# Modulation products issued a whole piece at a time, the half that lands last in front

## The chip, the cores and the metric

The kernel runs on one core of a Trainium2 chip. The metric is the device time of one execution in microseconds (us); runs of the kernel before and of the changed kernel are compared by it. The profile is one execution, taken by the hardware profiler, with the instructions of each engine: TensorE (PE for its matmuls, PEld for its weight loads), VectorE (DVE), ScalarE (ACT), GpSimd (POOL) and SyncE (SP), whose queue issues nearly all DMAs here.

## The reference

One layer of a hybrid backbone over 256 latent tokens of width 2048, with 256 context tokens beside them. What matters here is the modulation at its start:

```
mod   = silu(c)     @ ada_w + ada_b        # for the latent tokens
mod_c = silu(c_ctx) @ ada_w + ada_b        # for the context tokens
sh1, sc1, g1, sh2, sc2, g2 = split(mod, 6) # each 2048 wide
h  = rmsnorm(x)   * (1 + sc1)  + sh1
hc = rmsnorm(ctx) * (1 + csc1) + csh1
q, k, v, f, hy = split(h @ w_in)
kc, vc         = split(hc @ w_in[k and v columns])
```

After that come attention, a Fourier branch and a long-convolution branch, an output projection, a gated MLP and a final norm. They stand after the part that is changed here.

## The kernel before

The first stage computes `sh1` and `sc1` for both vectors at once and, from them, the projection to keys and values. The 2048 input columns are 16 tiles of 128 (`KT`), cut into five blocks of 2, 2, 4, 4 and 4 tiles (`CFG["blocks"]`). For each block the stage needs the modulation of that block's tiles (A and B, lines 502 and 503), then `hprep` (line 517) makes `h` and `hc` of these tiles as a high and a low part (`hx_hi`, `hx_lo`, `hc_hi`, `hc_lo`), and `group` (line 545) adds the block's share of keys and values. A block has four groups; the pieces of the next block's modulation are traced a quarter ahead of each group (lines 614 to 617).

A *piece* is what `piece(m, q)` returns, with `m` for scale (0) or shift (1). It loads two half-megabyte tiles of `ada_w` (`ada_load`, line 467, through the weight stream `load`, line 266), which are its two halves, and multiplies them with the two vectors `s_t`, which stand as the columns of a 128 x 32 stationary operand. The moving operand is 512 columns wide in blocks of four tiles and 256 in blocks of two. A piece of 512 columns has four products, a half two; a piece of 256 columns has eight, a half four. The product of input tile `kt` writes strip `kt % 4` of a PSUM bank, which is 32 partitions high; the four strips are added at the end, after the last piece of a scale or shift (lines 493 to 497: ScalarE copies the bank to `adasb`, TensorE transposes it, VectorE reduces it). A shift or scale takes four pieces at 512 columns and two at 256.

In all there are 4 pieces for block 0, which are worked in the start-up, 4 for block 1 and 8 each for blocks 2, 3 and 4.

The order on each engine is fixed when the kernel is built. The planner follows the order in which the program traces the instructions, but an instruction whose operands are not there yet by its estimate is passed by later ones that are ready. An edge between two instructions of one engine (`tc.issue_after`) says which is issued first; it adds no semaphore wait. On the chip each engine then runs its queue in that order, and an instruction waits on semaphores for what it reads. A product waits for the load of the half that it reads.

The buffers: eight half-megabyte tiles in `w1.raw`, which the modulation weights share with the projection weights (`w_kv_t`) and with the side products' weights (`ada_col_t`, line 351 on VectorE, which compute four other parts of the modulation and are drawn in by `pump`), and three more in `a_raw`. SP issues the loads in one order, and a load waits until its buffer is free, that is, until what read it is done.

## Time and profile before

| | us |
|---|---|
| median of three runs | 1309.89 |
| the three runs | 1307.58, 1309.89, 1340.22 |
| the profiled execution | 1307.8 |
| its span on the core | 1306.0 |
| TensorE busy (matmuls) | 1282.9 |
| VectorE busy | 887.3 |
| ScalarE busy | 557.7 |

The products of line 489 appear in the profile as `mi_ps<-raw,s_t` or, for block 0, `acc_ps<-raw,s_t`; the shape `128*32` is that of the stationary operand, `128x512` or `128x256` that of the moving one. The projection's matmuls appear on line 162, as `acc_ps<-hx_hi,w_hi` and the like. In a timeline row stand the start, the duration from the first record's start to the last one's end, the engine, the line, the operation, what it writes and reads, its shape and the number of records that were merged into the row, and in brackets the idle time of the engine before it and what ended that. Matmuls overlap in the pipeline, so the distance from one start to the next says more than a duration.

### The profile page before, as it was taken

How to read it: one execution, taken by the hardware profiler on the slowest of the kernel's cores; microseconds unless marked ns; L12 is line 12 of the kernel's file. 1: busy time of each engine (PE TensorE's matmuls, PEld its weight loads, DVE VectorE, ACT ScalarE, POOL GpSimd, SP SyncE). 2: the span in 40 equal slices, each digit the busy share in tenths (PEclk: the TensorE clock that was granted, in tenths of full speed). 3: DMA queues.
4: the chain of work that ended last, by engine and by line, in shares of the span. 5: the costliest groups of instructions: out<-in, count | busy, mean ns of one | idle time of the engine just before them, and what ended most of it. 6: DMA issues, size and time to landing. Idle time of an engine off the chain costs nothing.

```text
span 1306.0 us, 24498 instructions
## 1 busy us (share of the span) xinstructions
PE 1282.9 (98%) x10290; PEld 1195.4 (92%) x10290; DVE 887.3 (68%) x1301; ACT 557.7 (43%) x736; POOL 0.9 (0%) x7
## 2 busy tenths in 40 slices
PE   9899999999998999999999999999999999999997
PEld 5666787999998988999999999999999999999997
DVE  5435577977999897987767776744445555555563
ACT  3531223133443565555544444433334444454453
POOL 0000000000000000000000000000000000000000
PEclk9999999999999999999999999999999999999999
DMA  9976787988686875756777777855556656556541
GB/s 361 361 261 233 268 320 308 350 278 297 225 321 245 336 245 194 240 189 229 246 271 257 260 244 272 290 194 194 194 194 194 194 194 194 194 194 194 194 163 65
DMA packets 94015, 315.28 MB, mean 241 GB/s; under 512 B 16080, under 2 KB 16336, under 8 KB 93264
## 3 DMA queue, kind: packets, MB, share of 16 engines
q1 hardware_dynamic: 93328, 312.65, 68.8%
q8 instruction: 80, 1.31, 0.4%
q10 hardware_dynamic: 576, 1.07, 0.2%
q14 instruction: 31, 0.25, 0.1%
HBM read 311.58 MB, written 2.10 MB: 240 GB/s over the span
## 4 chain that ended last, share of the span: by engine, by line
PE 84%; DVE 9%; DMA 2%; ACT 2%; issue 2%; SPq 1%; DVEq 0%; ACTq 0%
PE acc_ps L162 77%; PE mi_ps L162 3%; PE mi_ps L489 3%; DVE raw L351 3%; DVE w_lo L174 2%; DMA raw<-in_ada_col_t 1%; SPq L636 1%; PE mi_ps L170 1%; DMA pack<-in_pack 0%; SPq L268 0%; DVE kT L570 0%; DVE v_t L570 0%; ACT w_hi L173 0%; ACT kT L461 0%; DVE Y L755 0%
## 5 line engine op out<-in xcount | busy, mean ns | idle before, releaser
L173 ACT CAST w_hi<-raw 128x1024 fp32r<-128x1024 f32 x376 | 380.5, 1050 | 514.1 <-PE acc_ps L162 467.4
L174 DVE TENSOR_TENSOR w_lo<-raw,w_hi 128x1024 fp32r<-128x1024 f32 x376 | 448.0, 1221 | 216.1 <-ACT w_hi L173 215.0
L162 PE MATMUL acc_ps<-h_hi,w_hi 128*128 128x256 f32 x1408 | 388.2, 276 | 0.5 <-ACT h_hi L256 0.5
L162 PE MATMUL acc_ps<-h_lo,w_hi 128*128 128x256 f32 x1408 | 388.6, 276 | 0.0
L162 PE MATMUL acc_ps<-h_hi,w_lo 128*128 128x256 f32 x1408 | 388.5, 276 | 0.0
L162 PEld LDWEIGHTS acc_ps<-h_hi,w_hi 128*128 128x128 f32 x1408 | 264.1, 188 | 0.7 <-ACT h_hi L256 0.7
L162 PEld LDWEIGHTS acc_ps<-h_lo,w_hi 128*128 128x128 f32 x1408 | 264.3, 188 | 0.0
L162 PEld LDWEIGHTS acc_ps<-h_hi,w_lo 128*128 128x128 f32 x1408 | 264.3, 188 | 0.0
L162 PE MATMUL acc_ps<-yh,w_lo 128*128 128x256 f32 x704 | 194.3, 276 | 0.0
L162 PE MATMUL acc_ps<-yh,w_hi 128*128 128x256 f32 x704 | 194.3, 276 | 0.0
L162 PE MATMUL acc_ps<-yl,w_hi 128*128 128x256 f32 x704 | 194.3, 276 | 0.0
L351 DVE SCALAR_TENSOR_TENSOR raw<-raw,s_row 128x1024 f32<-128x1024 f32 x128 | 154.4, 1220 | 35.1 <-DMA raw<-in_ada_col_t 35.0
L162 PE MATMUL acc_ps<-hx_hi,w_hi 128*128 128x256 f32 x512 | 143.6, 284 | 2.0 <-ACT hx_hi L256 2.0
L162 PE MATMUL acc_ps<-hx_hi,w_lo 128*128 128x256 f32 x512 | 142.9, 282 | 2.4 <-DVE w_lo L174 2.4
L162 PE MATMUL acc_ps<-hx_lo,w_hi 128*128 128x256 f32 x512 | 143.6, 282 | 0.0
L162 PEld LDWEIGHTS acc_ps<-yh,w_hi 128*128 128x128 f32 x704 | 132.2, 188 | 0.0
L162 PEld LDWEIGHTS acc_ps<-yl,w_hi 128*128 128x128 f32 x704 | 132.2, 188 | 0.0
L162 PEld LDWEIGHTS acc_ps<-yh,w_lo 128*128 128x128 f32 x704 | 132.2, 188 | 0.0
L162 PEld LDWEIGHTS acc_ps<-hx_hi,w_hi 128*128 128x128 f32 x512 | 96.5, 190 | 8.6 <-ACT hx_hi L256 4.0
L162 PEld LDWEIGHTS acc_ps<-hx_hi,w_lo 128*128 128x128 f32 x512 | 96.6, 190 | 6.7 <-issue 3.6
L162 PEld LDWEIGHTS acc_ps<-hx_lo,w_hi 128*128 128x128 f32 x512 | 97.3, 190 | 3.1 <-issue 2.2
L681 ACT ACTIVATE ga<-acc_ps,pack 128x256 f32<-128x256 f32 x44 | 23.7, 559 | 37.6 <-PE acc_ps L162 31.6
(237 smaller groups left out, 1532.9 us busy)
## 6 DMA issues: line engine op xcount, KB each, us to landing
raw<-in_ffn_t SPq DMA_DIRECT2D x264, 512.0 KB, 4.3
raw<-in_ada_col_t SPq DMA_DIRECT2D x128, 512.0 KB, 5.1
raw<-in_ada_t SPq DMA_DIRECT2D x64, 512.0 KB, 5.3
raw<-in_w_in_t SPq DMA_DIRECT2D x48, 512.0 KB, 5.8
raw<-in_w_kv_t SPq DMA_DIRECT2D x32, 512.0 KB, 5.9
raw<-in_w_out_t SPq DMA_DIRECT2D x32, 512.0 KB, 4.7
x_in<-in_xT SPq DMA_DIRECT2D x8, 256.0 KB, 5.4
kT<-in_c_tok SPq DMA_DIRECT2D x1, 2048.0 KB, 12.1
```

The lines of the kernel that those rows point to most:

```text
L162: return nc.tensor.matmul(ps, lhsT, rhs, start=start, stop=stop, skip_group_check=True)
L170: nc.tensor.transpose(ps, src, ident[:n, :n])
L173: nc.scalar.copy(hi, src)
L174: TT(lo, src, hi.bitcast(F32), op=ALU.subtract)
L351: STT(r, r, 1.0, s_row[:, h * NA : (h + 1) * NA], op0=ALU.mult, op1=ALU.mult, accum_out=sums_[:, f, h : h + 1])
L489: nc.tensor.matmul(ps[32 * j : 32 * j + 32, :w], s_t[:, kt, :], raws[(kt - n2 * q) // (n2 // 2)][:, kt % (n2 // 2), :], start=kt < 4, stop ...
L636: nc.sync.dma_start(half[:, hd], src)
L681: nc.scalar.activation(dst, ps, AF.Identity, bias=b, scale=w1_)
```

## The change

The products of a piece are issued in another order and tied together. The first product of the second half (the one that is loaded later) comes first; it waits for that half's load. All others of the piece, the rest of the second half and then the first half, are put behind it by `issue_after`. As the strips are now begun in another order, the flag that starts a strip's sum goes to the first product that touches the strip (`begun`), and the flag that ends it to the last ones. The loads, the buffers and the number of products stay as they are.

```diff
-                    for kt in range(n2 * q, n2 * q + n2):
+                    nh = n2 // 2
+
+                    def product(i):
+                        kt = n2 * q + i
                         j = kt % 4
-                        nc.tensor.matmul(ps[32 * j : 32 * j + 32, :w], s_t[:, kt, :], raws[(kt - n2 * q) // (n2 // 2)][:, kt % (n2 // 2), :], start=kt < 4, stop=kt >= KT - 4, skip_group_check=True)
+                        begun = st_.setdefault((m, "strips"), set())
+                        fresh = j not in begun
+                        begun.add(j)
+                        return nc.tensor.matmul(ps[32 * j : 32 * j + 32, :w], s_t[:, kt, :], raws[i // nh][:, kt % nh, :], start=fresh, stop=q == last_q and i in ends, skip_group_check=True)
+
+                    ends = range(4) if n2 == 8 else range(n2)
+                    last_raw = product(nh)
+                    with tc.issue_after(last_raw.ins):
+                        for i in [*range(nh + 1, n2), *range(nh)]:
+                            product(i)
                     if q < last_q:
                         return
```

## The prediction

> **What bounds the kernel now.** I read the page first, then the modulation products (line 489) by stretch, then single bursts of them in the timeline, then the loads that feed them.

> ```profile
> span 1306.0 us, 24498 instructions
> ...
> PE 1282.9 (98%) x10290; PEld 1195.4 (92%) x10290; DVE 887.3 (68%) x1301; ACT 557.7 (43%) x736; POOL 0.9 (0%) x7
> ...
> PE   9899999999998999999999999999999999999997
> ...
> DVE  5435577977999897987767776744445555555563
> ```

> TensorE is the bound: from the third slice on (a slice is 32.7 us) it is never below 80%, nearly always at 90% or more. What shortens TensorE's queue there can shorten the kernel, unless another engine steps in. The products stand in the first 215 us; the next view counts their records alone (the columns are the stretch, its length, TensorE's busy time and records, the clock, the DMA share, GB/s).

> ```profile
> 50.00:68.00 18.00, 5.11 (x64) 1.00 0.83 316
> 72.00:114.00 42.00, 16.83 (x64) 1.00 0.75 257
> 114.00:124.00 10.00, 4.21 (x16) 1.00 0.58 182
> 124.00:215.00 91.00, 13.46 (x112) 1.00 0.77 298
> ```

> One product is two records: the code issues 32 products of 256 columns for block 1 and the first row has 64. So 64, 64 + 16 and 112 records are 4, 20 and 7 bursts of 8, 4 and 16, sizes that the timeline shows. The 80 records of 72 to 124 us cost 21.04 us of busy time, the 112 after them 13.46: small bursts are dear. Why, one burst of four shows:

> ```profile
> 94.64 0.39 PE L162 MATMUL acc_ps<-w_lo,hx_hi 128*128 128x512 f32 x1
> 94.87 0.40 PE L162 MATMUL acc_ps<-w_hi,hx_lo 128*128 128x512 f32 x1
> 95.19 1.05 PE L489 MATMUL mi_ps<-raw,s_t 128*32 128x512 f32 x4
> 96.17 0.50 PE L162 MATMUL acc_ps<-w_hi,hx_hi 128*128 128x512 f32 x1
> 96.51 0.39 PE L162 MATMUL acc_ps<-w_lo,hx_hi 128*128 128x512 f32 x1
> ```

> Two projection matmuls follow one another in 0.23 us (94.64 to 94.87). From 94.87 to 96.51 two such steps should take 0.46; they take 1.64. The burst costs **1.18 us**: it enters 0.09 late, leaves 0.11 late, and ends with a tail that nothing fills.

> **The change, part by part.** What each step costs or saves:

> *Half pieces joined, 512 columns.* A whole piece uses all four strips of 32 output rows; a half uses two. What eight records (four products on four strips) take shows where two whole pieces are issued together. The first row below is cut at 131.20, so it holds the first piece only; the others are the whole burst.

> ```profile
> 130.63 1.06 PE L489 MATMUL mi_ps<-raw,s_t 128*32 128x512 f32 x8
> ```

> ```profile
> 130.43 0.28 PE L162 MATMUL acc_ps<-hc_hi,w_lo 128*128 128x256 f32 x1
> 130.63 1.92 PE L489 MATMUL mi_ps<-raw,s_t 128*32 128x512 f32 x16
> 132.49 0.38 PE L162 MATMUL acc_ps<-hx_hi,w_hi 128*128 128x256 f32 x1
> 132.71 0.28 PE L162 MATMUL acc_ps<-hx_lo,w_hi 128*128 128x256 f32 x1
> ```

> Four products on four strips last 1.06 us, two products on two strips 1.05. So the second half of a piece is free if it is issued beside the first: a joined piece costs 1.18 + 0.01 = 1.19 instead of 2 x 1.18 = 2.36, which saves **1.17**. The new order (third, fourth, first, second) still touches four different strips. The 20 bursts of four are 10 pairs: 11.7 us.

> [...]

> *Half pieces joined, 256 columns.*

> ```profile
> 50.63 0.28 PE L162 MATMUL acc_ps<-hx_lo,w_hi 128*128 128x256 f32 x1
> 50.84 0.64 PE L489 MATMUL mi_ps<-raw,s_t 128*32 128x256 f32 x8
> 51.41 0.38 PE L162 MATMUL acc_ps<-hx_hi,w_lo 128*128 128x256 f32 x1
> 51.63 0.29 PE L162 MATMUL acc_ps<-hx_hi,w_hi 128*128 128x256 f32 x1
> ```

> Here a half already uses four strips. From 50.63 to 51.63 two steps of 0.115 would do (256 columns, half of the 0.23 of 512); the burst costs 1.00 - 0.23 = 0.77. A whole piece of this width stands in the start-up:

> ```profile
> 24.69 1.50 PE L489 MATMUL acc_ps<-raw,s_t 128*32 128x256 f32 x22
> ...
> 30.06 1.05 PE L489 MATMUL acc_ps<-raw,s_t 128*32 128x256 f32 x10
> ...
> 34.67 1.07 PE L489 MATMUL acc_ps<-raw,s_t 128*32 128x256 f32 x16
> ```

> Sixteen records last 1.07, eight 0.64: 0.43 more. Joined 0.77 + 0.43 = 1.20 against 1.54 saves 0.34; four pairs, 1.4 us.

> *Start-up (block 0).* The third piece is split: six records ride in the burst of 22, ten come at 30.06. Whole, it would make 16 + 16: 0.43 off the first burst (1.50 to 1.07), 0.02 onto the second. After the first burst TensorE waits for ScalarE's copy of an earlier sum, so I take 0, with 0.4 as the upper bound.

> *The seven bursts of 16.* They are whole pieces already, two at a time; only their inner order changes. 0.

> *Cover that goes.* One removed burst, the one at 114.80, stands where TensorE waits for the next block's input:

> ```profile
> 114.22 0.66 PE L170 MATMUL mi_ps<-pack,adasb 128*128 128x128 f32 x4 [0.32 <-ACT adasb L493]
> 114.80 1.05 PE L489 MATMUL mi_ps<-raw,s_t 128*32 128x512 f32 x4
> ...
> 115.33 0.91 ACT L256 ACTIVATE hx_hi<-ht,B 128x256 fp32r<-128x256 f32 x2 [1.17 <-DVE B L503]
> ...
> 115.89 0.39 PE L162 MATMUL acc_ps<-hx_hi,w_hi 128*128 128x256 f32 x1
> ```

> The matmul at 115.89 waits for the activation of 115.33 whatever the burst does, so its removal uncovers an idle time of the same 1.1 us. That pair saves 0.1: minus 1.1.

> *The added wait.* A piece's first product now waits for the half that lands last, and behind it in TensorE's queue stand the other products and all projection matmuls. What they would wait:

> ```profile
> 56.95 2.31 SPq L268 DMA_DIRECT2D raw<-in_ada_t  x4
> ```

> ```profile
> DMA to landing us min/median/max: 3.4/4.3/8.7
> ```

> ```profile
> 72.34 1.05 PE L489 MATMUL mi_ps<-raw,s_t 128*32 128x512 f32 x4
> ...
> 78.42 1.05 PE L489 MATMUL mi_ps<-raw,s_t 128*32 128x512 f32 x4
> ```

> The four loads issued at 56.95 to 59.3 feed the four bursts from 72.34 to 78.42, so each is used 15 to 19 us after its issue. The second row is for loads of modulation weights issued between 50 and 125 us: they land within 8.7 us at worst. The wait has some 7 us to spare: 0.

> *Buffers held longer.* The first half's buffer is freed with the second half's burst instead of its own, which is 1.9 us later (93.31 against 95.19):

> ```profile
> 93.31 1.05 PE L489 MATMUL mi_ps<-raw,s_t 128*32 128x512 f32 x4
> ```

> ```profile
> SPq L268 <- PE mi_ps L489: 104.3, 29, 10.1
> ```

> SP's queue, in which all weight loads stand in one order, does wait for these releases (104.3 us in 29 waits up to 330 us), so loads will start later by up to 1.9. The 7 us spare covers it; I take 0 and price the opposite as the third rival. No load is moved in the program.

> *After it.* The gain arises before 124 us; does it reach the end?

> ```profile
> 125.00:222.00 97.00, 97.00 (x652) 77.69 (x651) 65.94 (x119) 22.50 (x33) 0.00 (x0) 1.00 0.79 307
> 222.00:285.00 63.00, 63.00 (x452) 58.73 (x452) 59.52 (x92) 16.18 (x18) 0.00 (x0) 1.00 0.90 325
> ```

> TensorE (first count) is full in both stretches, VectorE (third) has 31 us free in the first and only 3.5 in the second, DMA 10%. Both stretches are driven by releases of TensorE and VectorE, so they should shift as a whole.

> Sum: 11.7 + 1.4 + 0 - 1.1 = **12.0 us** less. Upper end: 0.4 in the start-up, and 1.7 if the two pieces of each of the five groups with bursts of four came together as later ones do (two joined pieces at 1.19 are 2.38, a burst of 16 costs 2.28 - 0.23 = 2.05 between 130.43 and 132.71: 0.33 x 5): 14.1. Lower end with one more burst found to be cover: 10.9; adding a pair whose order the planner keeps apart, 9.7. The profiled execution took 1307.8 us (span 1306.0, 1.8 around it), so it would take 1295.8. The median of three before is 1309.9, the lowest 1307.6; an ordinary run lies 0 to 2 above the profiled one, so I say **1297**.

> **The rivals.**

> *Gain given back later.* Between 222 and 285 us VectorE is busy 59.52 of 63 us, in queue order with side products that wait for loads. If it can't start 12 us earlier, up to half of the gain is lost: 1302. Against: its 31 free us in the stretch before. Chance 0.17.

> *The halves don't run beside one another.* Then a joined piece costs 1.18 + 0.87 = 2.05 (0.87 is what the burst of 16 has over the burst of four), a pair saves 0.31, ten 3.1, and with 1.4 and less 1.1 the time is 1304. The x8 row of 1.06 us speaks against it. Chance 0.05.

> *It does not do what it says.* The edges order products, they do not make them neighbours; if the planner still puts projection matmuls between them, the bursts stay as many: 1308 to 1310. Chance 0.06.

> *Slower: TensorE's queue stops at the front product.* The place is lines 489 and 268 between 50 and 215 us. The longer hold delays SP's next loads by 1.9 us for each of the 14 joined pieces; if these add up instead of being caught by the spare time, 26.6 us of TensorE waiting stand against 12 saved: 1322. It decides from the point at which the 7 us spare is used up, that is after four pieces whose delay isn't recovered. For it: SP does wait for line 489, 104.3 us in all. Against: in 50 to 124 us the DMA engines are busy 58 to 83%, so they can catch up. [...] Chance 0.11, of which 0.04 for more than 2% (a delay twice as long).

> *More than forecast*, below 1291, by changes of order that I can't read here: 0.05, of which 0.02 beyond 2%.

> **How the numbers follow.** The forecast, 1291 to 1299 (1307.8 less 14.1 or 9.7, and 1 to 3 us for what differs between runs), has 0.56; the first rival 0.17, the second 0.05, the third 0.06, slower 0.11, more 0.05. The range from 1290 to 1308 holds the forecast, the first two rivals and parts of the third and of the last: 8 in 10. A measurement here tells about 2% from no change (26 us: below 1284 or above 1336). All but 0.02 below and 0.04 above lies within: faster 0.02, same 0.94, slower 0.04.

> **What would show it.** Between 50 and 68 us bursts of 16 records instead of 8, and after that bursts of eight or 16 and none of four; 14 bursts fewer; a joined 512-column burst of about 1.06 us; an idle TensorE of about 1 us ahead of block 2's first projection; the first projection matmul after what is now the burst at 130.63 some 12 us earlier; the stretch now at 222 to 285 as long as before. Wrong would be: TensorE waiting for a load at line 489, bursts of four left, joined bursts near 2 us, or a VectorE wait after 222 us that grows by what was saved.

## The result and the profile after

The changed kernel takes **1300.03 us** (median of four runs, 1298.77 to 1302.15); the kernel before, run beside it, 1309.89. The ratio is 0.9923 with a 95% interval of 0.9899 to 0.9947: faster by 0.8%, less than the 2% that I had set as the bound. The profiled execution took 1298.77 us. Forecast were 1297 for an ordinary run and 1295.8 for the profiled one. Some executions of most kernels here, the kernel before included, run 25 to 32 us longer and are left out of all medians and ratios; the profiles of `two_strips`, `cover` and `pairs` are of such executions; their rows here lie, with one exception in the last section, in the first 135 us, and `pairs` is still level with the changed kernel between 215 and 295 us (546 projection matmuls against 547).

The page of the changed kernel, the lines that answer to those of before:

```profile
span 1297.0 us, 24499 instructions
...
PE 1271.9 (98%) x10290; PEld 1195.4 (92%) x10290; DVE 887.0 (68%) x1301; ACT 557.6 (43%) x736; POOL 0.9 (0%) x7
...
PE   9899999999989999999999999999999999999997
```

TensorE has the same 10290 records and is busy for 11.0 us less (1271.9 against 1282.9); the other engines do what they did. The products, now on line 495, by stretch (length, TensorE's busy time and records, clock, DMA share, GB/s):

```profile
54.00:69.00 15.00, 4.28 (x64) 1.00 0.84 306
72.00:114.00 42.00, 10.66 (x80) 1.00 0.86 304
114.00:120.00 6.00, 0.00 (x0) 1.00 0.87 310
120.00:202.00 82.00, 12.98 (x112) 1.00 0.77 303
```

The 80 records that cost 21.04 us before cost 10.66 now. The timeline of TensorE shows one burst of each size with its neighbours:

```profile
54.11 0.28 PE L162 MATMUL acc_ps<-hc_hi,w_hi 128*128 128x256 f32 x1
54.32 1.07 PE L495 MATMUL mi_ps<-raw,s_t 128*32 128x256 f32 x16
55.32 0.38 PE L162 MATMUL acc_ps<-hc_lo,w_hi 128*128 128x256 f32 x1
55.54 0.28 PE L162 MATMUL acc_ps<-hc_hi,w_lo 128*128 128x256 f32 x1
...
87.08 0.28 PE L162 MATMUL acc_ps<-hc_hi,w_hi 128*128 128x256 f32 x1
87.29 1.06 PE L495 MATMUL mi_ps<-raw,s_t 128*32 128x512 f32 x8
88.29 0.39 PE L162 MATMUL acc_ps<-hc_lo,w_hi 128*128 128x256 f32 x1
88.51 0.28 PE L162 MATMUL acc_ps<-hc_hi,w_lo 128*128 128x256 f32 x1
...
120.95 1.92 PE L495 MATMUL mi_ps<-raw,s_t 128*32 128x512 f32 x16
122.80 0.38 PE L162 MATMUL acc_ps<-hx_hi,w_hi 128*128 128x256 f32 x1
```

By the reading of the prediction, the joined piece of 512 columns costs 88.51 - 87.08 - 0.23 = 1.20 us (forecast 1.19), the one of 256 columns 55.54 - 54.11 - 0.23 = 1.20 (forecast 1.20). Between 50 and 120 us there are 4 bursts of 16 and 10 of eight where there were, up to 124 us, 8 of eight and 20 of four.

**Where the time went.** One and the same projection matmul, set against itself, at three places: a matmul shortly before block 1's products, one after them, and the one behind the first burst of block 4's. Kernel before:

```profile
49.81 0.28 PE L162 MATMUL acc_ps<-hx_hi,w_hi 128*128 128x256 f32 x1
...
72.02 0.39 PE L162 MATMUL acc_ps<-w_hi,hc_lo 128*128 128x512 f32 x1
```

Changed kernel:

```profile
51.84 0.28 PE L162 MATMUL acc_ps<-hx_hi,w_hi 128*128 128x256 f32 x1
...
72.65 0.39 PE L162 MATMUL acc_ps<-w_hi,hc_lo 128*128 128x512 f32 x1
```

The third matmul is the row at 132.49 of before and the row at 122.80 above. So the changed kernel is 2.03 us late at the first place, 0.63 late at the second and 9.69 early at the third: it gains 1.40 in block 1's pieces and 10.32 in those after them, 11.72 in all. At the end 9.0 are left (1306.0 less 1297.0): 11.72 gained, less 2.03 that were lost before the first place and 0.7 after the third.

### The profile page after: what moved, and what is told of

Its sections match the earlier page's. It is cut to its first block, busy times and chain, and to the rows that moved or that the text cites. A ratio compares the mean times of both kernels' runs of the same rounds, so it can differ in the third digit from the quotient of the medians.

```text
span 1297.0 us, 24499 instructions
## 1 busy us (share of the span) xinstructions
PE 1271.9 (98%) x10290; PEld 1195.4 (92%) x10290; DVE 887.0 (68%) x1301; ACT 557.6 (43%) x736; POOL 0.9 (0%) x7
## 3 DMA queue, kind: packets, MB, share of 16 engines
q10 hardware_dynamic: 576, 1.07, 0.2%
## 4 chain that ended last, share of the span: by engine, by line
PE 88%; DVE 6%; DMA 2%; SPq 1%; ACT 1%; issue 1%; DVEq 0%; ACTq 0%
PE acc_ps L162 82%; PE mi_ps L162 3%; PE mi_ps L495 2%; DVE w_lo L174 1%; SPq L648 1%; PE mi_ps L170 1%; DMA raw<-in_ada_col_t 1%; DVE raw L351 1%; DMA raw<-in_w_in_t 1%; SPq L268 0%; ACT w_hi L173 0%; DMA pack<-in_pack 0%; ACT kT L461 0%; DVE Y L767 0%; DVE X L774 0%
## 5 line engine op out<-in xcount | busy, mean ns | idle before, releaser
L162 PE MATMUL acc_ps<-h_hi,w_hi 128*128 128x256 f32 x1408 | 388.5, 276 | 0.5 <-ACT h_hi L256 0.5
L162 PE MATMUL acc_ps<-h_lo,w_hi 128*128 128x256 f32 x1408 | 388.8, 276 | 0.0
L162 PE MATMUL acc_ps<-h_hi,w_lo 128*128 128x256 f32 x1408 | 388.7, 276 | 0.0
L162 PEld LDWEIGHTS acc_ps<-h_hi,w_hi 128*128 128x128 f32 x1408 | 264.1, 188 | 0.7 <-ACT h_hi L256 0.7
L162 PEld LDWEIGHTS acc_ps<-h_lo,w_hi 128*128 128x128 f32 x1408 | 264.3, 188 | 0.0
L162 PEld LDWEIGHTS acc_ps<-h_hi,w_lo 128*128 128x128 f32 x1408 | 264.3, 188 | 0.0
L162 PE MATMUL acc_ps<-yh,w_lo 128*128 128x256 f32 x704 | 194.4, 276 | 0.0
L162 PE MATMUL acc_ps<-yl,w_hi 128*128 128x256 f32 x704 | 194.4, 276 | 0.0
L162 PE MATMUL acc_ps<-yh,w_hi 128*128 128x256 f32 x704 | 194.4, 276 | 0.0
L162 PE MATMUL acc_ps<-hx_hi,w_hi 128*128 128x256 f32 x512 | 142.9, 281 | 2.4 <-ACT hx_hi L256 2.4
L162 PE MATMUL acc_ps<-hx_hi,w_lo 128*128 128x256 f32 x512 | 141.9, 280 | 2.6 <-DVE w_lo L174 2.6
L162 PE MATMUL acc_ps<-hx_lo,w_hi 128*128 128x256 f32 x512 | 142.6, 280 | 0.0
L162 PEld LDWEIGHTS acc_ps<-yh,w_lo 128*128 128x128 f32 x704 | 132.2, 188 | 0.0
L162 PEld LDWEIGHTS acc_ps<-yh,w_hi 128*128 128x128 f32 x704 | 132.2, 188 | 0.0
L162 PEld LDWEIGHTS acc_ps<-yl,w_hi 128*128 128x128 f32 x704 | 132.2, 188 | 0.0
L162 PEld LDWEIGHTS acc_ps<-hx_hi,w_hi 128*128 128x128 f32 x512 | 96.1, 188 | 5.8 <-ACT hx_hi L256 2.9
L162 PEld LDWEIGHTS acc_ps<-hx_hi,w_lo 128*128 128x128 f32 x512 | 96.0, 189 | 5.3 <-DVE w_lo L174 3.4
L162 PEld LDWEIGHTS acc_ps<-hx_lo,w_hi 128*128 128x128 f32 x512 | 96.2, 188 | 1.5 <-DVE ht L252 0.8
## 6 DMA issues: line engine op xcount, KB each, us to landing
kT<-in_c_tok SPq DMA_DIRECT2D x1, 2048.0 KB, 10.9
```

Source lines behind the costliest of these rows:

```text
L162: return nc.tensor.matmul(ps, lhsT, rhs, start=start, stop=stop, skip_group_check=True)
```

## The experiments

**1. Two strips.** In the blocks of four tiles the second half is put on the same two strips as the first, so that a joined piece uses two strips instead of four; the number of bursts should stay.

```diff
-                        j = kt % 4
+                        j = kt % 4 if n2 == 8 else kt // 2 % 4
...
-                        for i in [*range(nh + 1, n2), *range(nh)]:
+                        for i in [*range(nh + 1, n2), *range(nh)] if n2 == 8 else [0, 3, 1]:
```

> The changed kernel, but in blocks of four tiles a piece's four products are laid on two strips (strip kt // 2 % 4 instead of kt % 4), two products on each. As many bursts as the changed kernel. Theory (the second half of a piece costs nothing because its two strips run beside the other two): a joined piece of 512 columns then takes two more passes of 0.43 us, about 1.85 us from its start to the next projection matmul instead of 1.00, 10 pieces, +8.6 us; the seven bursts of 16 take four more passes each, 3.57 instead of 1.85, +12.0 us; in all about 1320 to 1321 against 1300. [...]

Measured: 1308.2 us, ratio 0.9985 (0.997 to 0.9999). TensorE's timeline:

```profile
76.61 0.28 PE L162 MATMUL acc_ps<-hx_lo,w_hi 128*128 128x256 f32 x1
76.81 1.91 PE L495 MATMUL mi_ps<-raw,s_t 128*32 128x512 f32 x8
78.65 0.38 PE L162 MATMUL acc_ps<-hx_hi,w_lo 128*128 128x256 f32 x1
...
128.43 0.28 PE L162 MATMUL acc_ps<-hc_hi,w_lo 128*128 128x256 f32 x1
128.64 1.94 PE L495 MATMUL mi_ps<-raw,s_t 128*32 128x512 f32 x16
130.51 0.38 PE L162 MATMUL acc_ps<-hx_hi,w_hi 128*128 128x256 f32 x1
```

The joined piece takes 1.84 us to the next matmul (76.81 to 78.65) instead of 1.00 (87.29 to 88.29); ten of them are 8.4, and 1300.0 + 8.4 = 1308.4. The gain of joining is nearly gone though the bursts are as few. The expected 1320 was missed: the seven bursts of 16 stayed at 1.87 instead of doubling. By the edit the two pieces of such a burst lie on different pairs of strips, so all four strips were still in use; that the two pieces ran interleaved is read from the time alone, since no trace shows the strip of a record. What counts most is how many strips work beside one another, not the number of bursts.

**2. The order alone, 3. the edges alone.** The change has two parts; each is tried without the other.

```diff
-                    with tc.issue_after(last_raw.ins):
-                        for i in [*range(nh + 1, n2), *range(nh)]:
-                            product(i)
+                    for i in [*range(nh + 1, n2), *range(nh)]:
+                        product(i)
```

> The new order of the products alone: the half that lands last is traced first, without the edges that queue the others behind it. Theory that the edges join the pieces: as slow as before, 1310, with bursts of four between 72 and 124 us. Rival that the order does it, since products of one PSUM bank keep the order in which they are traced: as the changed kernel, 1300, no burst of four.

```diff
-                    last_raw = product(nh)
-                    with tc.issue_after(last_raw.ins):
-                        for i in [*range(nh + 1, n2), *range(nh)]:
+                    first_raw = product(0)
+                    with tc.issue_after(first_raw.ins):
+                        for i in range(1, n2):
```

> The edges alone: the products stay in the old order and are queued behind the first one. Theory that the edges join the pieces: 1300. Rival that the late half has to be in front: 1310, 20 bursts of four between 72 and 124 us as before, because the first half's products are still ready, and issued, a load earlier.

Measured: the order alone 1298.6 us, ratio 0.9911 (0.9883 to 0.994); the edges alone 1309.2, ratio 1.0001 (0.9983 to 1.002). TensorE's busy time on line 495 and its records between 50 and 124 us, order alone first, then edges alone (the first burst of block 4 falls into the former only, and the window cuts the last burst of the latter):

```profile
50.00:124.00 74.00, 17.02 (x160) 0.98 0.78 282
```

```profile
50.00:124.00 74.00, 25.36 (x142) 0.99 0.74 257
```

Without the edges TensorE, VectorE and ScalarE each run their instructions in the order of the changed kernel; with the edges alone, in that of the kernel before. The whole gain is in tracing the late half first; the edges add nothing here. Why the planner doesn't pass the early half forward once it is traced second, no trace tells; the rival's reason, that products of one bank keep the order in which they are traced, was not tried by itself.

**4. Pairs of pieces, 5. cover, 6. both.** If a joined piece saves, two pieces together should save once more, 0.33 us each by the prediction's bound (`pairs`). And the idle time of 1.0 us before block 2's first projection might be covered by the first products of block 3 (`cover`; `firsts[8]` is the last product of block 3's first burst). The core of the edits:

```diff
+            span = 2 if n2 == 4 else 1
...
-            def piece(m, q):
+            def piece(m, q0):
...
-                    last_raw = product(nh)
+                    q = q0 + span - 1
+                    last_raw = product(q, nh)
                     with tc.issue_after(last_raw.ins):
                         for i in [*range(nh + 1, n2), *range(nh)]:
-                            product(i)
+                            product(q, i)
+                        if span == 2:
+                            for i in range(n2):
+                                product(q0, i)
```

```diff
-                group(b, g)
+                with tc.issue_after(firsts[8].ins) if (b, g) == (2, 0) else ExitStack():
+                    group(b, g)
```

> The changed kernel with two pieces of 512 columns taken together, behind the load that lands last of their four: 12 bursts of 16 records in place of ten of 8 and seven of 16. Theory (a burst has a fixed cost of some 0.33 us beside its passes): five bursts fewer, 1.7 us less than the changed kernel. Rival (buffers held longer stop the loads: up to three half-megabyte buffers are held until the fourth lands): TensorE waits for loads at the products or the projection between 72 and 124 us, and the time is above 1300.

> The changed kernel with one more edge: block 2's first group of projection matmuls is queued behind the first piece of block 3, so that this burst stands where TensorE waits for block 2's input, and not 20 matmuls later. Theory (the change lost there the cover that the burst at 114.80 gave before): the wait of 1.02 us ahead of the first projection matmul is filled, the projection is 1.0 us earlier behind it, and no half-clock window follows; 1299 against 1300. Rival (the wait is not shortened, since the burst has to run anyway and the matmuls behind it wait for the next activation): unchanged, with the idle time moved to after the first four matmuls.

> Two pieces of 512 columns taken together, and the same edge: block 2's first group behind the first pair of block 3. Theory: a burst of 16 costs 2.05 us and 1.0 of it is covered; against the changed kernel 1.7 us from five bursts fewer and 1.0 from the cover, about 1297.5. Rival (four buffers held until the fourth load lands leave the loads too late): waits of TensorE for loads, 1300 or more.

Measured: `cover` 1299.4 us, ratio 0.9917 (0.9894 to 0.9941), no better than the change; `pairs_cover` 1295.8, ratio 0.9888 (0.9866 to 0.991). `pairs` has one time that counts, 1298.18, too few to compare; it was timed again, with the changed kernel and with both edits:

> The pieces of the blocks of four tiles two at a time, without the order of the next block's projection (the earlier timing of this kernel had one undisturbed run, 1298.2 us, and its trace showed 0.5 us gained over the changed kernel by 122 us). Theory (the join saves little by itself, since the burst at 100.89 us waits 0.85 us for the load of the later piece): 1298 to 1300, under 1 us from the changed kernel run beside it. Rival (a saved burst is worth 0.33 us in undisturbed runs too, six of them in all): 1.7 to 2 us under the changed kernel.

> The changed kernel once more, on the same chip as the two others: 1300 us, ratio to the kernel before 0.992; it is what the two others are set against.

> Two pieces at a time and block 3's first ones ahead of block 2's first group. Theory (both together gain 4 us, of which 1.6 were seen before 125 us in the trace): 1296, 4 us under the changed kernel beside it. Rival (the 4 us of the earlier timing were a difference between chips and executions): 1298 to 1299.

Measured on one chip: `pairs_again` 1298.4 us, ratio 0.9916 (0.9891 to 0.9942); `after_again` 1300.4, 0.9928 (0.9905 to 0.9951); `pairs_cover_again` 1296.4, 0.9907 (0.988 to 0.9934). The transition of the changed kernel, of `cover`, of `pairs_again` and of `pairs_cover_again`, in this order:

```profile
105.77 0.66 PE L170 MATMUL mi_ps<-pack,adasb 128*128 128x128 f32 x4 [0.79 <-ACT adasb L505]
...
106.89 0.91 ACT L256 ACTIVATE hx_hi<-ht,B 128x256 fp32r<-128x256 f32 x2 [1.17 <-DVE B L515]
...
107.44 0.38 PE L162 MATMUL acc_ps<-hx_hi,w_hi 128*128 128x256 f32 x1 [1.02 <-ACT hx_hi L256]
...
107.76 1.07 PE L495 MATMUL mi_ps<-raw,s_t 128*32 128x512 f32 x8
```

```profile
102.92 0.66 PE L170 MATMUL mi_ps<-pack,adasb 128*128 128x128 f32 x4 [0.79 <-ACT adasb L508]
...
103.51 1.06 PE L497 MATMUL mi_ps<-raw,s_t 128*32 128x512 f32 x8
...
104.60 0.38 PE L162 MATMUL acc_ps<-hx_hi,w_hi 128*128 128x256 f32 x1
...
106.45 0.39 PE L162 MATMUL acc_ps<-hx_hi,w_hi 128*128 128x256 f32 x1 [0.32 <-ACT hx_hi L256]
```

```profile
99.19 1.92 PE L497 MATMUL mi_ps<-raw,s_t 128*32 128x512 f32 x16
101.89 0.66 PE L170 MATMUL mi_ps<-pack,adasb 128*128 128x128 f32 x4 [0.78 <-ACT adasb L511]
```

```profile
103.70 0.66 PE L170 MATMUL mi_ps<-pack,adasb 128*128 128x128 f32 x4 [0.78 <-ACT adasb L514]
104.28 1.92 PE L499 MATMUL mi_ps<-raw,s_t 128*32 128x512 f32 x16
106.14 0.39 PE L162 MATMUL acc_ps<-hx_hi,w_hi 128*128 128x256 f32 x1
```

In `cover` the burst does fill the 1.02 us, and the projections that stood behind it move forward; but they use up the part of `h` that is there and then wait for ScalarE again (0.32 at 106.45), and by 125 us its lead over the changed kernel is what it was at 102 (2.89 against 2.84 us). In `cover` the chain from the sums over ScalarE and VectorE to `hx_hi` bounds this place; where the products stand beside it doesn't.

`pairs_again` is 2.0 us under `after_again`, but the intervals overlap. It has 20 bursts of products where the changed kernel has 25: five fewer, not the six of the expectation, which at 0.33 us are 1.65. The traces show less of it. From the second to the third matmul of "Where the time went" the changed kernel takes 50.2 us and `after_again` 50.7; `pairs` takes 49.8, `pairs_again` 49.4. So neither the theory (under 1 us) nor the rival is settled. My reason for the theory was wrong in any case: the wait before the row at 101.89 is for ScalarE's copy (`adasb`), not for a load, and the changed kernel has the same 0.79. With both edits the same stretch takes 48.6 and 49.2 us. `pairs_cover` has the lowest medians of all kernels here, some 4 us under the changed kernel (1295.8 and 1296.4; only the second was timed beside it), of which this stretch shows one to two. That both edits together do more than each alone is what the times say; that it is more than the difference between executions isn't settled.

**7. Fewer buffers.** Two of the eleven half-megabyte buffers are taken away.

```diff
-    a_raw = pool(p1s, "a_raw", 3, "right")
+    a_raw = pool(p1s, "a_raw", 1, "right")
```

> The changed kernel with one buffer instead of three in the second pool of weight tiles, nine half-megabyte buffers instead of eleven. Theory (the longer hold is caught by spare time: a half lands some 10 us before its products): two loads less in flight take 3 to 4 us of it, nothing waits, 1300. Rival (the longer hold has used the spare time up): products or casts wait for loads between 50 and 215 us, and the time is 1303 or more.

Measured: 1304.8 us, ratio 0.9953 (0.9936 to 0.9971): some two fifths of the gain are lost. The waits between 50 and 215 us (engine and line, releaser: us in total, times, longest), and SP's queue in the first 330 us; first of the kernel with fewer buffers, then of the changed kernel:

```profile
ACT w_hi L173 <- DMA raw<-in_w_kv_t: 16.1, 4, 5.5
...
PEld mi_ps L495 <- DMA raw<-in_ada_t: 4.4, 8, 1.2
...
SPq L268 <- PE mi_ps L495: 67.0, 23, 9.2
SPq L268 <- DMA raw<-in_ada_t: 51.3, 20, 4.9
```

```profile
SPq L268 <- PE mi_ps L495: 90.7, 23, 10.8
...
SPq L268 <- DMA raw<-in_ada_t: 5.7, 6, 1.5
```

With two buffers fewer the products wait for their loads in eight places, and the projection weights arrive late. In the changed kernel no burst of products starts on a load's landing between 50 and 215 us: the loads of each had landed 4.4 us or more before it, against 2.2 in the kernel before; both are bursts of block 4, and at the joined pieces it is 8.2 or more, against 7.9. So the spare time was there. But the edit changes more than the waits: with fewer buffers the planner also chose another order, with 30 bursts instead of 25, two of four records among them (71.64 and 73.91 us), and 18.1 us of TensorE on the products between 50 and 124 us instead of 16.9. How much of the loss is waiting and how much is this order, the run doesn't separate.

## Why the prediction was right, point by point

*Half pieces joined, 512 columns.* Forecast 1.17 a pair, ten pairs. A joined piece costs 1.20 instead of 1.19. `two_strips` shows that the reason is the right one: on two strips the same burst costs 0.84 more, and the time rises by about ten times that.

*Half pieces joined, 256 columns.* Forecast 1.4, measured 1.40 between the first and the second matmul above.

*Cover that goes.* Forecast minus 1.1. The row at 107.44 shows 1.02 us idle for `hx_hi`. Ten pairs less this were to bring 10.6; measured are 10.32. In `cover` block 3's first products stand there instead, and nothing is won back.

*The seven bursts of 16.* Forecast 0: 120.95 to 122.80 is 1.85, before 130.63 to 132.49 1.86.

*The added wait, the buffers held longer.* Forecast 0 each. No burst waits for a load, and SP's queue waits 90.7 us for the products' releases instead of 104.3. `one_a_raw` shows that the slower rival had a real limit behind it: with eleven buffers no product waits for a load, with nine they wait in eight places.

*After it.* The stretch that stood at 222 to 285 us, now 9.7 us earlier (the first count is TensorE, the third VectorE):

```profile
212.30:275.30 63.00, 63.00 (x439) 58.71 (x438) 59.63 (x92) 14.92 (x16) 0.00 (x0) 1.00 0.92 327
```

VectorE does the same 92 operations in the same 63 us, and TensorE doesn't wait for it: the rival "gain given back later" falls. But TensorE gets through 439 records where it got through 452, all the time busy. That is the slower pace of the last section; some 1.5 us go here, over half of which come back by the end.

*Half pieces that don't run beside one another*, *does not do what it says*: both fall, by the x8 burst of 1.06 us and by the count of bursts. *What bounds the kernel*: "from the third slice on never below 80%" overlooks the last slice of the page, which shows 7; the products stand far ahead of it.

**The term that missed in the profile** is the start-up: forecast 0 to 0.4 gained, found 2.03 us later by 51.84 us. The other profiles speak against the change as its cause. With the edges alone, whose engines run in the order of the kernel before, the matmul of 49.81 stands here:

```profile
52.15 0.28 PE L162 MATMUL acc_ps<-hx_hi,w_hi 128*128 128x256 f32 x1
```

The same order is 2.34 us later than in the profile of before. And `after_again`, which is the changed kernel, has that matmul 0.98 earlier than the changed kernel's own profile; the order alone, whose engines run in the same order, has it earlier still, 0.15 behind the kernel before:

```profile
50.86 0.28 PE L162 MATMUL acc_ps<-hx_hi,w_hi 128*128 128x256 f32 x1
```

```profile
49.96 0.28 PE L162 MATMUL acc_ps<-hx_hi,w_hi 128*128 128x256 f32 x1
```

The time of TensorE's slow windows in the start-up differs between executions: a granted clock of 0.50 stands at 38.87 to 42.28 us in the profile of before, at 47.84 to 51.25 in the changed kernel's. The profiled time of 1298.8 against the forecast 1295.8 is then 2.0 of start, 0.7 of pace and 0.3 of the sum of 12.0 that measured 11.7. The allowance of 1 to 3 us for what differs between runs covered this, though I had placed it after the sum and not in its first term.

**An ordinary run** gains less than the sum. The medians lie 9.9 us apart, and by the interval of the ratio the gain is 6.9 to 13.2 us. 1300.03 is one microsecond above the 1291 to 1299 of the forecast itself; it falls into the stated range because that reached up to 1308 for the rivals, and none of these happened. From the first to the third matmul the changed kernel's profile gains 11.7 us, `after_again` 11.2, the order alone 10.0 with a slow window in this stretch. Two of these three then lose 1.5 behind the third matmul. In the changed kernel's profile the slower pace falls there (439 records of TensorE from 212.3 to 275.3 us), in that of the kernel before it doesn't (452 from 222 to 285). Whether that is chance, these few profiles can't tell.

## What to carry to other kernels

Eight records on four strips of 32 output rows took 1.06 us here and on two strips 1.91, so issue such products as many strips at a time as there are: look in the timeline for bursts that last as long with half the records, and trace first the one whose operand lands last. Weigh a removed burst against the wait that it stood beside; here one of the ten gave nothing back. A sum of single bursts can be right to 0.3 us where two profiles of the same order differ by 2, so set the same instruction against itself at several places before explaining a total.

## What the runs showed of the hardware

**Four strips in one pass.** Eight records on four strips took 1.06 us (the changed kernel, 87.29 us), eight on two strips 1.91 (`two_strips`, 76.81), and four on two strips 1.05 (the kernel before, 95.19). Four records more cost 0.01 us on the two other strips and 0.86 on the same two.

**Slow windows of the clock.** With the order alone, this stood right behind the transition to block 2 (stretch, length, busy time of PE, PEld, DVE, ACT and POOL, clock, DMA share, GB/s):

```profile
103.35:106.76 3.41, 1.74 (x13) 0.76 (x13) 1.53 (x6) 1.49 (x3) 0.00 (x0) 1.00 0.93 321
106.76:110.17 3.41, 3.41 (x18) 3.02 (x15) 3.05 (x8) 2.25 (x5) 0.00 (x0) 0.50 0.94 300
110.17:113.58 3.41, 3.41 (x29) 2.45 (x29) 3.41 (x7) 2.35 (x4) 0.00 (x0) 1.00 0.22 49
```

After 3.41 us in which TensorE was busy for 1.74, the granted clock was 0.50 for the next 3.41 us; 18 matmul records went through in these, 29 in the 3.41 us behind them at a clock of 1.00. The changed kernel had the same idle times (0.79 and 1.02) and no such window there. The slow windows ahead of its last matmul begin at 47.84 and 389.17 us, 341.33 apart, those of the kernel before at 38.87 and 397.27, 358.40 apart; by the clock records of the two traces each lasts 3.413 us at 0.50, and the distances are 100 and 105 times that, to within 0.04 us. Counted on from the end of the changed kernel's first (51.25 us) in steps of this length, its idle times fall into two stretches:

```profile
102.45:105.86 3.41, 2.62 (x16) 1.18 (x15) 1.38 (x2) 0.58 (x1) 0.00 (x0) 1.00 0.88 263
105.86:109.27 3.41, 2.39 (x17) 1.18 (x18) 2.11 (x7) 1.44 (x4) 0.00 (x0) 1.00 0.95 334
```

```profile
46.00:51.00 5.00, 4.24 (x37) 4.11 (x41) 3.28 (x6) 4.55 (x8) 0.00 (x0) 1.00 0.99 405
```

```profile
46.00:51.00 5.00, 3.72 (x19) 3.72 (x20) 3.15 (x6) 2.99 (x6) 0.00 (x0) 0.68 1.03 419
```

In the changed kernel the window fell onto projections that were ready to run, and half as many got done (19 records against 37).

**Two paces of one matmul.** Records of line 162 in 100 us of the gated MLP, changed kernel, then the first execution of `pairs`:

```profile
700.00:800.00 100.00, 100.00 (x884) 1.00 0.75 256
```

```profile
700.00:800.00 100.00, 100.00 (x852) 1.00 0.74 248
```

At a full granted clock and without a wait, the matmuls of 256 columns follow one another, from start to start, in 113.3 ns in the one and 117.8 in the other. In shorter stretches the paces change within an execution: between 212.3 and 275.3 us the changed kernel ran at the slower one (118 ns from start to start in the median, in the kernel before 113 to 114 between 222 and 285). What sets the pace, no run here shows.
